# One encoder layer on one core: sums of the down weights formed in the gate/up part and kept in DRAM, operands loaded in pairs, four gate products run ahead, and the norm of the first four token tiles inside the last pass

## Chip, cores and metric

One NeuronCore of a Trainium2 chip runs the whole layer in one launch. The metric is the device time in microseconds; the median of three runs is given beside the lowest and the highest.

## What is computed

The input x is 1024 tokens by 1024 channels in float32. The layer is a half-step SwiGLU, a mixer, another half-step SwiGLU and a last norm:

```
x = x + 0.5 * swiglu(rmsnorm(x, ff1_norm), ff1_w_gate, ff1_w_up, ff1_w_down)
h = rmsnorm(x, mix_norm);  proj = h @ w_in
x = x + merged(gMLP(proj), stick_breaking_attention(proj)) @ w_out
x = x + 0.5 * swiglu(rmsnorm(x, ff2_norm), ff2_w_gate, ff2_w_up, ff2_w_down)
y = rmsnorm(x, final_norm)
swiglu(x, g, u, d) = (silu(x @ g) * (x @ u)) @ d        # d_ff = 2816
```

The change touches the two SwiGLU stages alone, "the first half" (stage f1, whose next consumer is the mixer) and "the second half" (stage f2, whose next consumer is the output).

## The kernel before, in words

Every operand of a matmul is split in two float32r parts, hi (a cast by ACT, L73) and lo (source minus hi by DVE, L74), and each product is three matmuls, hi·hi, hi·lo and lo·hi (`mm3f`, L170 to L172). A pair of such parts of a 128x512 block is a *form* (`form`).

Each SwiGLU stage (`ffn`) multiplies 2x2 blocks by Strassen's scheme in Winograd's form, with seven products instead of eight, and so needs sums and differences of blocks on both sides.

*Prologue* (`right_forms`): eight token tiles of 128 tokens are loaded (xr, two buffers), normed (`normed`, `rstd`), transposed by PE (nt, L203, eight transposes a tile) and written as the right operands B11, B21 (tiles 0 to 3) and T1 to T4, B22 (tiles 4 to 7, differences with tiles 0 to 3, which are kept in `keep`). `rstd` squares on ACT (L105), adds on DVE (L107, L108) and takes the power on POOL (L109). With `offload` one half of the norm is a product on POOL (L116) that ACT scales (L120); the other half is one DVE instruction (L122).

*Gate/up part*: 22 column tiles f of 128 columns. `head(f)` loads 512 KB of gate and of up weights (raw, four buffers) and does the first two products; `tail(f)` does the sums of weights (ws) and the other five, 84 matmuls of 512 columns together. Two heads run ahead. SiLU and the product with up (`gated`) give the activation blocks (act); after every second f, DVE forms the sums S1 to S4 (as, three buffers) and SP writes seven blocks of 256 KB to DRAM.

*Down part*: four passes over 11 pairs j of row blocks. Pass 1 is A11·B11 + A12·B21 in eight PSUM banks (A and B), pass 2 S2·T2 and S1·T1, pass 3 S3·T3 and S4·B22, pass 4 A22·T4 in four banks. Passes 1 to 3 have 24 matmuls per j, pass 4 has 12: 924 in all. The forms live in eight buffers for even j (wf) and eight for odd j (pf). T1 to T4 are formed here, by DVE from rows of the down weights (L367, L368, L381, L400); T2 goes to DRAM after pass 2 and comes back in pass 4. Between passes DVE drains the banks into x (L359, L360, L375, L376, L389 to L391). Then `after(t)` norms the tiles 0 to 3; in the first half it also transposes them for the mixer (L142) and writes x to DRAM. In pass 4 the last five j run token tile by token tile, and each tile is drained (L408) and normed when its bank is done.

```
            def pair(*srcs):
                r = bp.tile([P, D], F32, tag="raw", bufs=4, name="raw")
                for i, src in enumerate(srcs):
                    nc.sync.dma_start(out=r[:, i * HALF:(i + 1) * HALF], in_=src)
                return cut(r)
```

All DMAs stand in one queue, SP's, and each engine takes its instructions in one fixed order. The framework orders them when the program is built, from the order of the code and the buffers that are free; so a line that stands late in the code can stand early in a queue. An instruction that waits holds all behind it on its engine.

Of the kernel before, what the change touches and what calls it, by code (L numbers as in the profile page):

```python
# [32 lines left out]
class Kernel:  # L33
# [78 lines left out]
    def normed(self, x, gain, tiles, offload):  # L112

        nc = self.nc
        if offload:
            nc.gpsimd.tensor_tensor(tiles[1], x[1], gain[1], op=ALU.mult)  # L116
        r = self.rstd(x)
        for i in range(2):
            if offload and i == 1:
# [13 lines left out]
    def norm_t(self, x, t, gain, h, split=True):  # L133
# [4 lines left out]
        self.normed(x[t], gain, xns, split)  # L138
        for i, xn in enumerate(xns):
            ps = self.psum("p2" if split else ("p2", "p1")[i], "nt")  # L140
# [33 lines left out]
    def right_forms(self, xsrc, gain_src, tp):  # L174


        nc, tt = self.nc, self.nc.vector.tensor_tensor
        names = ("B11", "B21", "T2", "T1", "T3", "T4", "B22")
        T = {n: (self.hp if i < 4 else tp).tile([P, 4, 2, HALF], F32R, tag="h", name=n) for i, n in enumerate(names)}
        with self.tc.tile_pool(name="pre", bufs=1, reuse_waits="tile") as pre:  # L180
            tmp = lambda tag, bufs: pre.tile([P, HALF], F32, tag=tag, bufs=bufs, name=tag)
            self.np_ = pre
            xs = []
# [9 lines left out]
            nc.sync.dma_start(out=gain, in_=gain_src.partition_broadcast(P))  # L193
            for t in range(NT):
                x, nxt = nxt, load(t + 1) if t + 1 < NT else None
                xn = [tmp("xn", 3) for _ in range(2)]
                cut = lambda y: [y[:, i * HALF:(i + 1) * HALF] for i in range(2)]
                self.normed(cut(x), cut(gain), xn, t >= 4)
# [7 lines left out]
                r3 = lambda y: y.rearrange("p (k c) -> p k c", k=4)  # L206

                def put(name, src):
                    o = T[name]
                    self.split(o[:, :, 0, c:c + P], o[:, :, 1, c:c + P], r3(src))  # L210

                if t < 4:
                    for i, name in enumerate(("B11", "B21")):
                        put(name, n[i])
                        keep[i, t] = tmp("keep", 8)
                        nc.scalar.copy(keep[i, t], n[i])
                else:
                    t1, t2, t3, t4 = (tmp("t", 3) for _ in range(4))
# [3 lines left out]
                    put("T1", t1)  # L222
                    tt(t2, n[1], t1, op=ALU.subtract)
                    put("T2", t2)
                    tt(t3, n[1], b12, op=ALU.subtract)
                    put("T3", t3)
                    put("B22", n[1])
                    tt(t4, t2, keep[1, t - 4], op=ALU.subtract)
                    put("T4", t4)
        return T  # L230

    def ffn(self, xsrc, gain_src, wg, wu, wd, before, after):

        nc, tc, tt = self.nc, self.tc, self.nc.vector.tensor_tensor
        nff, nj = DFF // P, DFF // P // 2
        aform = {n: self.dram.tile([nj * P, HALF], F32, name=f"{self.stage}_{n}") for n in ("A11", "A12", "A22", "S1", "S2", "S3", "S4")}
        t2dram = self.dram.tile([nj * P, HALF], F32, name=f"{self.stage}_t2")
        with ExitStack() as outer:
            fps = outer.enter_context(tc.tile_pool(name="fps", bufs=8, space=PSUM, reuse_waits="tile"))
            self.psum = lambda tag, name: fps.tile([P, HALF], F32, tag="ps", name=name)  # L240
            bp = outer.enter_context(tc.tile_pool(name="bp", bufs=1, reuse_waits="tile"))


            with tc.tile_pool(name="tp", bufs=3, reuse_waits="tile") as tp:
                T = self.right_forms(xsrc, gain_src, tp)
                with tc.tile_pool(name="pa", bufs=1, reuse_waits="tile") as pa:
                    tile = lambda tag, bufs: pa.tile([P, HALF], F32, tag=tag, bufs=bufs, name=tag)

                    def weights(f):
                        raw = []  # L250
                        for w in (wg, wu):
                            r = bp.tile([P, D], F32, tag="raw", bufs=4, name="raw")
                            nc.sync.dma_start(out=r.rearrange("p (k c) -> p k c", k=NK), in_=w[:, f * P:(f + 1) * P].rearrange("(k p) c -> p k c", p=P))
                            raw += [r[:, :HALF], r[:, HALF:]]
                        return raw
# [7 lines left out]
                    def head(f):  # L263

                        raw = weights(f)
                        b, a = self.psum("ps", "pb"), self.psum("ps", "pa")
                        product(b, raw[0], "B11", True)
                        p1 = tile("pe", 4)
                        nc.scalar.copy(p1, b)
                        product(a, raw[1], "B21", True)  # L270
                        glo = tile("gs", 4)
                        tt(glo, a, p1, op=ALU.add)
                        return raw, b, glo

                    def gated(g, u):

                        s = tile("gs", 4)
# [5 lines left out]
                    def tail(f, raw, b, glo):  # L283
                        a11, a12, a21, a22 = raw
                        s1, s2, s3, s4 = self.sums(lambda: tile("ws", 4), *raw)
                        product(b, s2, "T2", False)
                        w = tile("pe", 4)
# [4 lines left out]
                        v = tile("pe", 4)  # L292
# [8 lines left out]
                        ghi = tile("gs", 4)  # L301
# [3 lines left out]
                    heads = {f: head(f) for f in range(2)}  # L305
                    for f in range(nff):
                        out = tail(f, *heads.pop(f))
                        if f % 2 == 0:
                            even = out
                        else:  # L310
                            j = f // 2
                            blocks = dict(zip(("A11", "A12", "A21", "A22"), (even[0], out[0], even[1], out[1])))
                            blocks |= zip(("S1", "S2", "S3", "S4"), self.sums(lambda: tile("as", 3), *blocks.values()))
                            for n, dst in aform.items():
                                nc.sync.dma_start(out=dst[j * P:(j + 1) * P, :], in_=blocks[n])
                        if f + 2 < nff:
                            heads[f + 2] = head(f + 2)


            with tc.tile_pool(name="pb", bufs=1, reuse_waits="tile") as pb:  # L320
# [3 lines left out]
                cut = lambda y: [y[:, i * HALF:(i + 1) * HALF] for i in range(2)]  # L324
                wdq = lambda j, r, c: wd[(2 * j + r) * P:(2 * j + r + 1) * P, c * HALF:(c + 1) * HALF]
                af = lambda n, j: aform[n][j * P:(j + 1) * P, :]
# [442 lines left out]
```

## Time and profile before

| | us |
|---|---|
| median of 3 runs | 2624.23 |
| lowest, highest | 2623.71, 2625.22 |
| the profiled execution, its own time | 2623.44 |
| its span | 2621.7 |
| PE busy | 2446.7 (93%) |
| DVE busy | 1724.2 (66%) |
| ACT busy | 1054.5 (40%) |
| POOL busy | 306.5 (12%) |

The span is one execution as the profiler saw it, 1.7 us less than the time of the same execution. PE is the busiest engine. Busy time of PE is modelled for pipelined matmuls: a matmul of 512 columns shows some 390 ns, but one issues about every 227 ns. An engine's idle time costs nothing unless the chain of waits runs through it.

### The profile page before, as it was taken

To read this page: it belongs to the slowest core of one execution; us is meant where nothing else is said; L and a number is where in the kernel's file an instruction comes from. 1 tells how busy PE (TensorE), PEld (TensorE's weight loads), DVE (VectorE), ACT (ScalarE), POOL (GpSimd) and SP (SyncE) were. 2 spreads that over 40 slices of the span, in tenths; PEclk is the share of its full clock that TensorE was granted. 3 is DMA by queue.
4 is the path that set the end of the run, shared out by engine and by line. 5 is a ranking of instruction groups with operands and counts; after the bars stand their busy time and mean duration, and the time that the engine had idled before them with its cause. 6 is when DMAs were issued, how large, how long until landed. Compare 5 with 4: busy or idle time off the path is not lost.

```text
span 2621.7 us, 33247 instructions
## 1 busy us (share of the span) xinstructions
PE 2446.7 (93%) x12140; PEld 2073.0 (79%) x12140; DVE 1724.2 (66%) x2641; ACT 1054.5 (40%) x2004; POOL 306.5 (12%) x478
## 2 busy tenths in 40 slices
PE   4999999999689999999999999999959999999987
PEld 3888888787477989888888888888748888887875
DVE  7777676575647888878766555145586766765756
ACT  6333333433335666666522222221063333333334
POOL 1000000000104454544300000000010000000002
PEclk9999999999799999999999999999969999999998
DMA  3332333785422122121121122123232333337754
GB/s 113 97 116 94 99 114 109 269 293 167 138 73 69 43 57 55 43 57 49 33 57 53 47 69 62 56 72 105 98 103 89 121 101 101 101 114 277 264 172 164
DMA packets 258755, 282.67 MB, mean 108 GB/s; under 512 B 16801, under 2 KB 165793, under 8 KB 258593
## 3 DMA queue, kind: packets, MB, share of 16 engines
q1 hardware_dynamic: 258592, 280.56, 33.8%
q8 instruction: 95, 1.56, 0.2%
q14 instruction: 68, 0.55, 0.1%
HBM read 209.20 MB, written 62.91 MB: 104 GB/s over the span
## 4 chain that ended last, share of the span: by engine, by line
PE 75%; DMA 11%; DVE 8%; issue 3%; ACT 2%; SPq 1%; POOL 1%; DVEq 0%; POOLq 0%; ACTq 0%
PE pj L67 7%; PE pj L69 7%; PE pj L68 7%; DMA raw<-in_ff_w_down_dram 6%; PE pb L171 5%; PE pb L170 5%; PE pb L172 5%; PE pd L171 3%; PE pd L170 3%; PE pd L172 3%; PE av L524 3%; PE pv L68 2%; PE pv L69 2%; PE pv L67 2%; PE tr L517 2%
## 5 line engine op out<-in xcount | busy, mean ns | idle before, releaser
L67 PE MATMUL pj<-h,wr 128*128 128x512 f32 x640 | 252.5, 395 | 6.9 <-DVE q L74 6.9
L69 PE MATMUL pj<-h,wr 128*128 128x512 f32 x640 | 250.8, 392 | 0.1
L68 PE MATMUL pj<-h,wr 128*128 128x512 f32 x640 | 250.6, 392 | 0.0
L74 DVE TENSOR_TENSOR wf<-raw,wf 128x512 fp32r<-128x512 f32 x252 | 170.9, 688 | 111.4 <-ACT wf L73 111.0
L73 ACT CAST wf<-raw 128x512 fp32r<-128x512 f32 x252 | 153.0, 621 | 192.8 <-PE pa L172 61.4
L500 DVE TENSOR_TENSOR_SCAN kp<-kp 128x128 f32<-128x128 f32 (+7 forms) x128 | 181.8, 1426 | 44.7 <-POOL kp L498 43.1
L73 ACT CAST wf<-ws 128x512 fp32r<-128x512 f32 x176 | 109.2, 623 | 139.2 <-PE pd L172 128.0
L170 PE MATMUL pd<-wf 128*128 128x512 f32 x336 | 134.8, 401 | 26.1 <-DVE x L375 15.7
L56 DVE TENSOR_TENSOR wr<-raw,wr 128x1024 fp32r<-128x1024 f32 x80 | 97.9, 1223 | 81.8 <-ACT wr L55 81.6
L504 POOL TENSOR_TENSOR bt<-bt,kp 128x512 f32<-128x512 f32 (+4 forms) x128 | 133.8, 1046 | 131.4 <-DVE kp L500 104.8
L67 PE MATMUL pv<-wr,h 128*128 128x256 f32 x512 | 145.9, 287 | 1.9 <-ACT vg L566 1.9
L68 PE MATMUL pv<-wr,h 128*128 128x256 f32 x512 | 145.4, 284 | 0.6 <-DVE wr L56 0.6
L69 PE MATMUL pv<-wr,h 128*128 128x256 f32 x512 | 145.2, 284 | 0.0
L67 PEld LDWEIGHTS pj<-h,wr 128*128 128x128 f32 x640 | 120.6, 189 | 31.0 <-DVE q L74 7.6
L69 PEld LDWEIGHTS pj<-h,wr 128*128 128x128 f32 x640 | 120.5, 188 | 25.2 <-DVE wr L56 0.3
L68 PEld LDWEIGHTS pj<-h,wr 128*128 128x128 f32 x640 | 120.8, 189 | 23.4
L170 PE MATMUL pb<-T,wf 128*128 128x512 f32 x352 | 136.9, 389 | 0.0
L171 PE MATMUL pb<-T,wf 128*128 128x512 f32 x352 | 136.9, 389 | 0.0
L172 PE MATMUL pb<-T,wf 128*128 128x512 f32 x352 | 136.9, 389 | 0.0
L55 ACT CAST wr<-raw 128x1024 fp32r<-128x1024 f32 x80 | 84.2, 1052 | 130.1 <-PE pd L69 53.6
L171 PE MATMUL pd<-wf 128*128 128x512 f32 x336 | 134.0, 399 | 0.3 <-DVE wf L74 0.2
L172 PE MATMUL pd<-wf 128*128 128x512 f32 x336 | 133.2, 398 | 0.0
(210 smaller groups left out, 6488.2 us busy)
## 6 DMA issues: line engine op xcount, KB each, us to landing
raw<-in_ff_w_down_dram SPq DMA_DIRECT2D x132, 256.0 KB, 4.0
raw<-in_w_in_dram SPq DMA_DIRECT2D x56, 512.0 KB, 3.9
raw<-in_ff_w_gate_dram SPq DMA_DIRECT2D x44, 512.0 KB, 5.5
raw<-in_ff_w_up_dram SPq DMA_DIRECT2D x44, 512.0 KB, 4.0
f_S<-as SPq DMA_DIRECT2D x88, 256.0 KB, 2.1
raw<-f_S SPq DMA_DIRECT2D x88, 256.0 KB, 4.2
f_A<-act SPq DMA_DIRECT2D x66, 256.0 KB, 3.3
raw<-f_A SPq DMA_DIRECT2D x66, 256.0 KB, 3.8
```

Source lines behind the costliest of these rows:

```text
L55: nc.scalar.copy(wr[:, 0, :], raw)
L56: (nc.gpsimd if early else nc.vector).tensor_tensor(wr[:, 1, :], raw, wr[:, 0, :].bitcast(F32), op=ALU.subtract)
L67: mm(ps, lhsT=lh, rhs=rh, start=first, stop=False)
L68: mm(ps, lhsT=lh, rhs=rl, start=False, stop=False)
L69: mm(ps, lhsT=ll, rhs=rh, start=False, stop=last)
L73: self.nc.scalar.copy(hi, src)
L74: self.nc.vector.tensor_tensor(lo, src, hi.bitcast(F32), op=ALU.subtract)
L170: mm(ps, lhsT=lh, rhs=rh, start=first, stop=False, skip_group_check=True)
L171: mm(ps, lhsT=lh, rhs=rl, start=False, stop=False, skip_group_check=True)
L172: mm(ps, lhsT=ll, rhs=rh, start=False, stop=last, skip_group_check=True)
L500: nc.vector.tensor_tensor_scan(rev, rev, rev, 1.0, op0=ALU.mult, op1=ALU.bypass)
L504: eng.tensor_tensor(bt[:, :n], bt[:, :n], kp[:, i * HALF + 1:i * HALF + 1 + n], op=ALU.mult)
```

## The change

In the gate/up part, `right_sums(j)` loads two whole down rows after every even f, forms T1 to T4 on DVE and writes them to DRAM; `left_sums(j)` writes S2 with S1 and S3 with S4 as one block of 512 KB each. The DRAM layout puts the two operands that a pass needs together side by side, so that `pair` loads 512 KB at once. Four heads run ahead instead of two; for these the gate weights are loaded a second time, and from f = 4 on a head stands directly ahead of its tail. In the prologue both halves of the norm are DVE's, POOL takes three of five low parts of tiles 4 to 7 and the sum `keep`, which ACT copied before. In the down part the sums are gone, the fourth pass starts ahead of the norm, and the norm of tiles 0 to 3 (both halves offloaded to POOL and ACT) stands inside it.

```diff
@@ normed: offload is now the number of halves that go to POOL and ACT
-        if offload:
-            nc.gpsimd.tensor_tensor(tiles[1], x[1], gain[1], op=ALU.mult)
+        far = [i for i in range(2) if i >= 2 - offload]
+        for i in far:
+            nc.gpsimd.tensor_tensor(tiles[i], x[i], gain[i], op=ALU.mult)
@@ right_forms
-                self.normed(cut(x), cut(gain), xn, t >= 4)
+                self.normed(cut(x), cut(gain), xn, 0)
...
-                        put(name, n[i])
+                        hi, lo = put(name, n[i], tt)
                         keep[i, t] = tmp("keep", 8)
-                        nc.scalar.copy(keep[i, t], n[i])
+                        pt(r3(keep[i, t]), hi, lo, op=ALU.add)
                 else:
...
+                    put("T2", t2, tt)
+                    put("T1", t1, pt)
...
+                    put("T3", t3, pt)
+                    put("B22", n[1], tt)
                     tt(t4, t2, keep[1, t - 4], op=ALU.subtract)
+                    put("T4", t4, pt)
@@ ffn
-        nff, nj = DFF // P, DFF // P // 2
+        nff, nj, nhead = DFF // P, DFF // P // 2, 4
+        scratch = {n: self.dram.tile([nj * P, D], F32, name=f"{self.stage}_{n}") for n in ("a11a12", "s2s1", "s3s4", "a22t4", "t2t1", "t3")}
...
-                    def tail(f, raw, b, glo):
-                        a11, a12, a21, a22 = raw
+                    def tail(f, gate, b, glo):
+                        a11, a12 = weights(wg, f) if f < nhead else gate
+                        a21, a22 = weights(wu, f)
...
+                    def left_sums(j, a11, a12, a21, a22):
+                        s21, s34 = pairs()
+                        self.sums(iter((s21[:, HALF:], s21[:, :HALF], s34[:, :HALF], s34[:, HALF:])).__next__, a11, a12, a21, a22)
+                        for n, i, y in (("a11a12", 0, a11), ("a11a12", 1, a12), ("a22t4", 0, a22), ("s2s1", None, s21), ("s3s4", None, s34)):
+                            nc.sync.dma_start(out=dst(n, j, i), in_=y)
+                    def right_sums(j):
+                        r = [rawt() for _ in range(2)]
+                        for i in range(2):
+                            nc.sync.dma_start(out=r[i], in_=wd[(2 * j + i) * P:(2 * j + i + 1) * P, :])
+                        (b11, b12), (b21, b22) = cut(r[0]), cut(r[1])
+                        t21, t34 = pairs()
+                        (t2, t1), (t3, t4) = cut(t21), cut(t34)
+                        tt(t1, b12, b11, op=ALU.subtract)
+                        tt(t2, b22, t1, op=ALU.subtract)
+                        tt(t3, b22, b12, op=ALU.subtract)
+                        tt(t4, t2, b21, op=ALU.subtract)
+                        for n, i, y in (("t2t1", None, t21), ("t3", 0, t3), ("a22t4", 1, t4)):
+                            nc.sync.dma_start(out=dst(n, j, i), in_=y)
-                    heads = {f: head(f) for f in range(2)}
+                    heads = {f: head(f) for f in range(nhead)}
                     for f in range(nff):
-                        out = tail(f, *heads.pop(f))
+                        out = tail(f, *(heads.pop(f) if f in heads else head(f)))
                         if f % 2 == 0:
                             even = out
+                            right_sums(f // 2)
...
+                def pair(src):
+                    r = rawt() if len(src) == 1 else pb.tile([P, D], F32, tag="rw", bufs=3, name="rw")
+                    for i, y in enumerate(src):
+                        o = r if len(src) == 1 else r[:, i * HALF:(i + 1) * HALF]
+                        nc.sync.dma_start(out=o if len(y.shape) == 2 else o.rearrange("p (r c) -> p r c", r=2), in_=y)
                     return cut(r)
+                two(lambda j: [dst("a11a12", j)], lambda j: [col1(j)], A, B, "AB")
...
+                two(lambda j: [dst("s2s1", j)], lambda j: [dst("t2t1", j)], A, B, "B")
...
+                two(lambda j: [dst("s3s4", j)], lambda j: [dst("t3", j, 0), b22(j)], A, B, "")
...
+                old, A, fs = A, banks(), {}
+                last(range(3), range(4))
                 for t in range(4):
+                    tt(xh(t + 4, 0), old[t], xh(t + 4, 0), op=ALU.add)
+                    tt(xh(t + 4, 1), old[t], xh(t + 4, 1), op=ALU.add)
+                after(0, cut(x[0]), cut(gain), 2)
+                after(1, cut(x[1]), cut(gain), 2)
+                last(range(3, 6), range(4))
+                after(2, cut(x[2]), cut(gain), 2)
+                after(3, cut(x[3]), cut(gain), 2)
+                for t in range(4):
+                    last(range(6, nj), [t], t == 0)
                     tt(xh(t + 4, 0), xh(t + 4, 0), A[t], op=ALU.subtract)
+                    after(t + 4, cut(x[t + 4]), cut(gain), 1)
```

`two` is the loop of passes 1 to 3 with its operands as arguments: `pair` for the left and for the right, four forms, and the 24 matmuls of before. In passes 1 and 2 both loads are whole, in pass 3 the right one is two halves in the pool rw. In the changed kernel the line numbers shift: L388 and L389 drain after pass 2, L395, L407 and L408 after pass 3, L416 after pass 4.

How the queues stand is shown at three places. The first is SP's queue from the start of the first half, ahead of the loads of the gate/up part. Before:

```order
L188 DMA xr<-in_x_dram 128x1024
L193 DMA gain<-in_ff_norm_dram 128x1024
L188 DMA xr<-in_x_dram 128x1024
L253 DMA raw<-in_ff_w_gate_dram 128x8x128
L253 DMA raw<-in_ff_w_up_dram 128x8x128
L253 DMA raw<-in_ff_w_gate_dram 128x8x128
L253 DMA raw<-in_ff_w_up_dram 128x8x128
L676 DMA bgate<-in_b_gate_dram 128x16x1
L188 DMA xr<-in_x_dram 128x1024 x6
```

And of the change:

```order
L188 DMA xr<-in_x_dram 128x1024
L193 DMA gain<-in_ff_norm_dram 128x1024
L188 DMA xr<-in_x_dram 128x1024
L260 DMA raw<-in_ff_w_gate_dram 128x8x128 x4
L684 DMA bgate<-in_b_gate_dram 128x16x1
L188 DMA xr<-in_x_dram 128x1024
L260 DMA raw<-in_ff_w_gate_dram 128x8x128
L260 DMA raw<-in_ff_w_up_dram 128x8x128
L188 DMA xr<-in_x_dram 128x1024
L326 DMA raw<-in_ff_w_down_dram 128x1024 x2
L188 DMA xr<-in_x_dram 128x1024 x4
```

Four more loads of 512 KB stand ahead of token tile 4: the reload of the first gate weights, the first up weights and two down rows. In the second half the reload stands ahead of tile 0, and the up weights and two down rows ahead of tile 2.

The second place is DVE's queue between passes 2 and 3 of the first half; the forms wf and pf with a source raw, wt or rw are those of passes 2 and 3, and L375 and L388 are the drains of bank group A. Before:

```order
L381 TENSOR_TENSOR wt<-raw 128x512
L74 TENSOR_TENSOR pf<-raw,pf 128x512
L74 TENSOR_TENSOR pf<-wt,pf 128x512
L74 TENSOR_TENSOR pf<-raw,pf 128x512 x2
L74 TENSOR_TENSOR wf<-raw,wf 128x512
L74 TENSOR_TENSOR wf<-wt,wf 128x512
L381 TENSOR_TENSOR wt<-raw 128x512
L74 TENSOR_TENSOR wf<-raw,wf 128x512 x2
L74 TENSOR_TENSOR pf<-raw,pf 128x512
L375 TENSOR_TENSOR x<-pd,x 128x512
L376 TENSOR_TENSOR x<-pd,x 128x512
L381 TENSOR_TENSOR wt<-raw 128x512
```

And of the change:

```order
L74 TENSOR_TENSOR pf<-raw,pf 128x512
L74 TENSOR_TENSOR pf<-rw,pf 128x512
L74 TENSOR_TENSOR wf<-raw,wf 128x512
L74 TENSOR_TENSOR wf<-rw,wf 128x512
L74 TENSOR_TENSOR wf<-raw,wf 128x512
L74 TENSOR_TENSOR wf<-rw,wf 128x512
L74 TENSOR_TENSOR pf<-raw,pf 128x512
L74 TENSOR_TENSOR pf<-rw,pf 128x512
L388 TENSOR_TENSOR x<-pd,x 128x512
L74 TENSOR_TENSOR pf<-raw,pf 128x512
L389 TENSOR_TENSOR x<-pd,x 128x512
L74 TENSOR_TENSOR pf<-rw,pf 128x512
```

The subtractions L381 are gone from the queue ahead of the drains and between them, and the forms of two j of pass 3 stand ahead of the first drain.

The third place is PE's queue in the first half around the first transposes of the norm (nt). Before, they stand between pass 3 and pass 4:

```order
L170 MATMUL pd<-wf 128x512
L171 MATMUL pd<-wf 128x512
L172 MATMUL pd<-wf 128x512
L142 MATMUL nt<-ident,xn 128x128 x32
L170 MATMUL pd<-wf 128x512
L171 MATMUL pd<-wf 128x512
```

And of the change:

```order
L173 MATMUL pd<-pf 128x512
L171 MATMUL pd<-pf 128x512
L143 MATMUL nt<-ident,xn 128x128 x8
L172 MATMUL pd<-pf 128x512
L173 MATMUL pd<-pf 128x512
L171 MATMUL pd<-wf 128x512
```

The eight transposes of tile 0 now stand behind 67 matmuls of pass 4; those of tiles 1 to 3 follow within the next 49, and those of tiles 4 to 7 stand behind its last matmul.

## Rows read from the trace of the kernel before

**Rows 1.** Windows: us, busy of PE, PEld, DVE, ACT, POOL, PEclk, DMA share, GB/s.
```profile
0.00:52.00 52.00, 15.46 (x64) 12.43 (x65) 36.35 (x66) 34.96 (x75) 10.94 (x18) 1.00 0.45 132
52.00:475.50 423.50, 423.50 (x1865) 350.61 (x1864) 296.24 (x470) 157.08 (x274) 0.00 (x0) 1.00 0.33 104
475.50:749.00 273.50, 226.70 (x978) 185.99 (x977) 170.93 (x272) 110.20 (x207) 15.63 (x16) 0.90 0.63 212
1895.00:1948.60 53.60, 15.46 (x64) 12.45 (x65) 37.19 (x67) 33.91 (x74) 10.21 (x12) 0.53 0.43 138
1948.60:2372.00 423.40, 423.40 (x1862) 350.56 (x1861) 296.18 (x470) 155.77 (x273) 0.00 (x0) 1.00 0.32 103
2372.00:2621.70 249.70, 216.34 (x913) 175.63 (x912) 159.92 (x254) 99.18 (x188) 15.75 (x16) 0.93 0.65 223
```

**Rows 2.** Timeline of PE: start, length, instruction, idle before and its ender.
```profile
483.84 0.79 PE L171 MATMUL pd<-pf 128*128 128x512 f32 x1 [3.52 <-DVE pf L74]
607.04 0.76 PE L170 MATMUL pd<-wf 128*128 128x512 f32 x1 [6.28 <-DVE x L375]
689.92 1.97 PE L142 MATMUL nt<-ident,xn 128*128 128x128 f32 x8 [20.95 <-DVE xn L122]
2578.33 0.76 PE L170 MATMUL pd<-wf 128*128 128x512 f32 x1 [8.81 <-DVE x L389]
```

**Rows 3.** Waits of PE: waited for, us in total, times, longest.
```profile
PE pd L170 <- DVE x L375: 15.7, 2, 9.5
```

**Rows 4.** Chain of waits, pass 4, first half: start, us, what.
```profile
702.88 0.43 PE pd L170
706.89 0.23 PE pd L171
```

**Rows 5.** Timeline of DVE at the starts of pass 1 and pass 3.
```profile
481.89 0.69 DVE L165 TENSOR_TENSOR as<-act,as 128x512 f32<-128x512 f32 x1 [1.42 <-DMA f_S<-as]
600.94 0.69 DVE L381 TENSOR_TENSOR wt<-raw 128x512 f32<-128x512 f32 x1 [3.25 <-DMA raw<-in_ff_w_down_dram]
606.21 0.69 DVE L375 TENSOR_TENSOR x<-pd,x 128x512 f32<-128x512 f32 x1
606.81 0.68 DVE L376 TENSOR_TENSOR x<-pd,x 128x512 f32<-128x512 f32 x1
```

**Rows 6.** Timeline of PE in the prologues: one token tile's transposes.
```profile
36.93 1.94 PE L203 MATMUL nt<-ident,xn 128*128 128x128 f32 x8 [3.81 <-DVE xn L122]
44.19 1.94 PE L203 MATMUL nt<-ident,xn 128*128 128x128 f32 x8 [5.32 <-DVE xn L122]
50.43 1.94 PE L203 MATMUL nt<-ident,xn 128*128 128x128 f32 x8 [4.31 <-DVE xn L122]
1947.01 1.94 PE L203 MATMUL nt<-ident,xn 128*128 128x128 f32 x8 [4.30 <-DVE xn L122]
```

**Rows 7.** Timeline of DVE and of POOL, late token tiles of the first prologue.
```profile
30.29 0.74 DVE L122 SCALAR_TENSOR_TENSOR xn<-xr,rs,gain 128x512 f32<-128x512 f32 x1
35.02 1.76 DVE L122 SCALAR_TENSOR_TENSOR xn<-xr,rs,gain 128x512 f32<-128x512 f32 x1
34.62 1.61 POOL L116 TENSOR_TENSOR xn<-xr,gain 128x512 f32<-128x512 f32 x1
```

**Rows 8.** Timeline of PE at the end of the two halves.
```profile
735.33 1.03 PE L142 MATMUL nt<-ident,xn 128*128 128x128 f32 x8
746.64 1.97 PE L142 MATMUL nt<-ident,xn 128*128 128x128 f32 x8 [4.42 <-DVE xn L122]
2612.04 0.39 PE L172 MATMUL pd<-wf 128*128 128x512 f32 x1
```

**Rows 9.** DMA issues: queue, count, KB each, median us from issue to landing.
```profile
raw<-in_w_in_dram SPq DMA_DIRECT2D x56, 512.0 KB, 3.9
raw<-f_S SPq DMA_DIRECT2D x88, 256.0 KB, 4.2
```

**Rows 10.** View by windows, pass 1 while x is loaded.
```profile
490.00:540.00 50.00, 49.56 (x219) 40.73 (x217) 27.61 (x44) 21.46 (x38) 0.00 (x0) 1.00 0.95 325
```

More of the change, by code (lines that the diff above doesn't have):

```diff
@@ L241, in ffn @@
             bp = outer.enter_context(tc.tile_pool(name="bp", bufs=1, reuse_waits="tile"))
+            rawt = lambda: bp.tile([P, D], F32, tag="raw", bufs=4, name="raw")
             with tc.tile_pool(name="tp", bufs=3, reuse_waits="tile") as tp:
@@ L247, in ffn, with weights @@
                     tile = lambda tag, bufs: pa.tile([P, HALF], F32, tag=tag, bufs=bufs, name=tag)
[L249 to L255, printed above, removed]
+                    def weights(w, f):
+                        r = rawt()
+                        nc.sync.dma_start(out=r.rearrange("p (k c) -> p k c", k=NK), in_=w[:, f * P:(f + 1) * P].rearrange("(k p) c -> p k c", p=P))
+                        return cut(r)
                     def product(ps, src, right, first, last=True):
@@ L263, in head @@
                     def head(f):
-                        raw = weights(f)
+                        gate = weights(wg, f)
                         b, a = self.psum("ps", "pb"), self.psum("ps", "pa")
-                        product(b, raw[0], "B11", True)
-                        p1 = tile("pe", 4)
+                        product(b, gate[0], "B11", True)
+                        p1 = tile("pe", 3)
                         nc.scalar.copy(p1, b)
-                        product(a, raw[1], "B21", True)
-                        glo = tile("gs", 4)
+                        product(a, gate[1], "B21", True)
+                        glo = tile("gs", 6)
                         tt(glo, a, p1, op=ALU.add)
-                        return raw, b, glo
+                        return gate, b, glo
                     def gated(g, u):
-                        s = tile("gs", 4)
+                        s = tile("gs", 6)
                         nc.scalar.activation(s, g, AF.Sigmoid)
@@ L300, in tail, with pairs @@
                         lo = gated(glo, ulo)
-                        ghi = tile("gs", 4)
+                        ghi = tile("gs", 6)
                         tt(ghi, d, w, op=ALU.add)
                         return lo, gated(ghi, uhi)
-                    heads = {f: head(f) for f in range(2)}
+                    def pairs():
+                        return [pa.tile([P, D], F32, tag="as", bufs=3, name="as") for _ in range(2)]
+                    def left_sums(j, a11, a12, a21, a22):
[3 more added lines that the diff above has]
+                            nc.sync.dma_start(out=dst(n, j, i), in_=y)
```

133 lines of the change are left out of this document (41 added, 92 removed).

## Prediction, made before the changed kernel ran

> **What bounds the kernel now.** I read the stages first. In both gate/up parts PE is busy all of the time, 423.5 us of 423.5 for 1865 recorded matmuls, so a matmul of 512 columns issues every 0.227 us [rows 1]. These parts can't get shorter while their matmuls stay. PE's losses lie elsewhere: two prologues of some 52 us, in which PE does 15.5 us of transposes, and two down parts of 273.5 and 249.7 us [rows 1] that hold 924 matmuls each, 924 x 0.227 = 209.7 us.
>
> PE's timeline names the holes of the down parts [rows 2]. At the start of pass 1 it idles 3.5 us for the low part of a form. At the start of pass 3 it idles 6.3 us for a bank that DVE has not drained (L375), and 9.5 us in the second half, since the two waits sum to 15.7 [rows 3]. Ahead of pass 4 it idles 21.0 us in the first half, for the norm of token tile 0, whose transposes stand ahead of pass 4 in PE's queue, and 8.8 us in the second, where nothing is transposed [rows 2]. After a hole the matmuls issue every 0.43 us for some ten of them before they return to 0.23 [rows 4]: some 10 x 0.20 = 2 us more each time. That is the lower level of the granted clock, 1.2 GHz for 2.4.
>
> Why DVE is late shows in its own timeline [rows 5]. The drain L375 at 606.21 stands behind L381, a subtraction that waited 3.25 us for a row of down weights. The sum L165 waited 1.42 us for the write of an earlier sum out of the same three buffers. So transfers bound these starts, through DVE's queue. A 512 KB load lands in 3.9 us, a 256 KB one in 4.2 [rows 9]: two halves cost more than one whole.
>
> **Removed: the sums in passes 2 to 4.** L381 and its like leave DVE's queue; pass 3's operands are one whole load and two halves prefetched in a pool of three. The DVE order shows two tiles' forms ahead of the drains now, 48 matmuls or 10.9 us of cover, and nothing there waits for raw down weights to be subtracted. Both holes go: 6.3 + 9.5, and 2 of slow matmuls each, **-19.8 us**. Bounds: 0 if the paired loads come as late, 19.8 if they don't.
>
> **Moved: the norm of the first four tiles.** In the first half pass 3 ends at 689.92 - 20.95 = 668.97, and the last transposes end at 746.64 + 1.97 = 748.6 [rows 2, 8], 79.6 us later. In the new order pass 4 needs only the drains of B, which begin before pass 3 ends; I allow 1.5 us. Its 132 matmuls take 30.0 us, four tiles' transposes at 1.03 each 4.1 [rows 8], and the tail from 735.33 on stays, 13.3 [rows 8]: 48.9, a gain of 30.7. In the second half the old stretch runs from 2578.33 - 8.81 = 2569.5 to 2621.7, 52.2 us [rows 2]. The new one is 1.5 + 30.0 and the tail after the last matmul, 2621.7 - 2612.4 = 9.3 [rows 8]: 40.8, a gain of 11.4. The norm's price is that it now runs beside the forms. It brings twelve POOL products into the pass. One such product, 1.61 us at 34.62, goes with a DVE instruction of 1.76 us at 35.02 that takes 0.74 alone [rows 7], so each may cost DVE 1.0 us: 0 to 12 us per half. I take 3, since tile 0's transposes stand behind 67 matmuls (15 us of cover): **-27.7 and -8.4 us**.
>
> **Start of pass 1.** The 1.42 us wait for the sum's buffer goes, but only 6 matmuls stand between the last gate/up product and the first form of the next tile. The sigmoid, two products and four sums still come first on DVE. I take **-2 us** for both halves (bounds 0 and 11: 3.5 of idle time and 2 of slow matmuls each).
>
> **Added: sums of down weights in the gate/up part.** Forty-four subtractions per half, 44 x 0.60 = 26 us of DVE at the interval between 606.21 and 606.81 [rows 5], where DVE is busy 296 of 423.5 us [rows 1]. In the steady stretch it is 70% and becomes 76%, hidden. But after four early pairs of products come four tails of 60 matmuls, 13.6 us each, and such a tail costs DVE 16 instructions plus 4 sums, 20 x 0.60 = 12.0 us: 88%, where a late transfer has little slack. I take **+2 us** per half (bounds 0 and 6). The traffic grows by 2 MB per pair of columns in 38 us, far under the 325 GB/s that pass 1 sustains [rows 10].
>
> **Prologues.** Running four pairs ahead gains nothing by itself: in both orders all 64 transposes stand ahead of the first product, and PE does not idle after it [rows 1]. What counts is when the last transposes run, 50.43 and 1947.01 [rows 6]. A late tile takes 7.26 us now (36.93 to 44.19), on DVE. It then has eight DVE instructions of 0.60 and two short ones for the statistics, some 5.1 us, and POOL three subtractions at up to 1.61 us [rows 7] and the power. If POOL never holds DVE the three periods save 3 x 2 = 6 us; if each of its three does for 1.0, a period is 8.2 and they lose 3. I take 7.0. Against it, SP's order puts a reload, the up weights and two down rows, 2 MB or 6.5 us at 325 GB/s [rows 10], ahead of the x tile 4 that starts this stretch; in the second half three of the four. I take **+3 and +1 us** (bounds -6 and +9 each).
>
> The Trainium skill (SBUF — State Buffer, Who interferes with whom) states that a DVE instruction with two SBUF inputs and a GpSimd instruction that reads SBUF shut each other out for the whole instruction. The 1.76 against 0.74 [rows 7] agrees, and the rule speaks against moving subtractions to POOL: four of DVE's eight still have two SBUF inputs. By it these four and the three of POOL run one after the other, 4 x 0.60 + 3 x 1.61 = 7.2 us a tile, so the sum would be 3 x 0.2 = 0.6 us longer per prologue than by my 7.0.
>
> **The sum.** -19.8 - 27.7 - 8.4 - 2 + 4 + 4 = -49.9. The profiled execution took 2623.4 us (span 2621.7), 0.8 under the median of the three runs. I predict **2573.5 us**.
>
> **Rivals.** *One: the prologue becomes POOL's and SP's.* If every POOL subtraction shuts out DVE, a period is 8.2 or more and the x tiles come 6.5 us later, so each prologue ends 9 us late: 2573.5 + 14 = 2587.5. For it: rows 7, and the order of SP. Against it: most POOL subtractions can run beside drains from PSUM. Chance 0.18. *Two: the norm within pass 4 makes PE wait.* If its twelve POOL products cost DVE 12 us per half, and PE stops at the transposes, 18 us of the 36 are lost: 2591.5. Against it: the cover of 15 us. Chance 0.13. *Three, slower: the sums wait in the gate/up part.* Each of the 22 groups of subtractions needs two down rows that SP issues behind writes which wait for DVE; all forms stand behind the subtractions. If each group stops PE, it costs about a landing of 4.2 us [rows 9], 22 x 4.2 = 92: 2666. It turns the sign from 50 / 22 = 2.3 us of stall per group on. Against it: four load buffers and 24% of DVE free. Chance 0.06. *Four: the change doesn't do what it says,* because paired loads come as late as halves did and the drains stand behind them; then the 19.8 stays, and with a half of the pass-4 gain gone too the time is 2611. Chance 0.06. My forecast has 0.57.
>
> **How the numbers follow.** Forecast, rivals one, two and four are faster: 0.94, less 0.03 for the parts of one, two and four in which further losses stack, of which 0.02 is no change and 0.01 slower. A measurement of this kernel tells 0.2% from no change, 5 us. So faster 0.91, same 0.02, slower 0.07. The range starts where all bounds of the down parts go well and the prologues save 3 each: 2573.5 - 6 (norm) - 4 (pass 1) - 10 (prologues as above, -3 for +3 and +1) = 2553. It ends above rivals one and two, at 2604, with part of rival four outside.
>
> **What would show it.** PE's wait for L375's successor L388 near zero; the idle time before pass 4 under 2 us in both halves; PE 100% busy in the gate/up parts; the prologues' last transposes at about 53 and 50 us after their start. The prediction is wrong if PE waits for DVE in the gate/up parts, if the transposes inside pass 4 are preceded by idle time, or if the prologues end later than 60 us.

## The result and the profile after

The changed kernel takes 2588.89 us (median of 4 runs, 2588.20 to 2589.35), the kernel before in the same comparison 2624.72 (2623.71 to 2626.21). The ratio is 0.9863, with a 95% interval of 0.9846 to 0.988: 1.4% faster, 36 us where 50 were forecast. The profiled execution has a span of 2587.6 us (2621.7 before).

Busy time by stage of the kernel after, each stage from one mark to the next (columns as in [rows 1]). The marks are the first product of the gate/up part, the matmul that ends the wait for the first low part in pass 1, the first matmul of the mixer and its last:

```profile
core 0: us, PE busy (x) PEld busy (x) DVE busy (x) ACT busy (x) POOL busy (x), PEclk, DMA share, GB/s
0.00:63.26 63.26, 15.95 (x64) 12.17 (x65) 45.79 (x68) 30.74 (x68) 29.44 (x31) 1.00 0.47 141
63.26:495.83 432.57, 428.44 (x1879) 353.18 (x1877) 322.23 (x514) 162.46 (x279) 4.58 (x3) 1.00 0.48 158
495.83:719.93 224.10, 215.31 (x960) 177.88 (x961) 130.83 (x214) 105.54 (x200) 20.34 (x20) 0.96 0.62 214
719.93:1872.04 1152.11, 1132.45 (x6406) 991.55 (x6404) 728.02 (x1046) 463.62 (x916) 259.93 (x416) 0.99 0.20 58
1872.04:1941.07 69.03, 16.30 (x66) 12.16 (x65) 48.01 (x68) 29.88 (x67) 27.87 (x25) 0.53 0.44 137
1941.07:2373.43 432.36, 428.24 (x1878) 353.13 (x1876) 321.85 (x514) 160.91 (x278) 4.59 (x3) 0.99 0.48 158
2373.43:2587.60 214.17, 205.71 (x896) 169.76 (x896) 118.48 (x196) 95.39 (x183) 20.32 (x20) 0.98 0.61 214
```

The same marks in the kernel before give the table that the rest of this text uses; each column is one profiled execution. The forecast column sorts the prediction's terms into these stages (1 us of the -2 for pass 1 goes to each gate/up part; +3 and +1 to the prologues; -8.3 and -11.5 of the -19.8 to the two down parts).

| stage | before | after | difference | forecast |
|---|---|---|---|---|
| prologue 1 | 52.0 | 63.3 | +11.2 | +3 |
| gate/up 1 and start of pass 1 | 431.8 | 432.6 | +0.8 | +1 |
| rest of down part 1 | 264.4 | 224.1 | -40.3 | -36.0 |
| mixer | 1146.2 | 1152.1 | +5.9 | 0 |
| prologue 2 | 54.1 | 69.0 | +14.9 | +1 |
| gate/up 2 and start of pass 1 | 432.4 | 432.4 | 0.0 | +1 |
| rest of down part 2 | 240.7 | 214.2 | -26.5 | -19.9 |
| sum | | | -34.1 | -49.9 |

The down parts gave more than forecast. The loss lies in the prologues, and in a stage that the change doesn't touch. PE's longest waits after (engine, line, releaser: total, times, longest) answer to [rows 3] and [rows 2]:

```profile
PE nt L204 <- DVE xn L123: 100.0, 22, 17.0
PE nt L143 <- DVE xn L123: 7.8, 3, 4.0
PE pd L172 <- DVE pf L74: 5.5, 2, 2.7
PE pd L171 <- ACT pf L73: 2.1, 2, 1.1
```

No drain stands in the list any more: the holes of 6.3 and 9.5 us at the start of pass 3 and of 8.8 us ahead of pass 4 are gone. The prologue's wait for the norm (L204) grew instead, from 74.8 to 100.0 us. PE's timeline of the changed kernel holds these idle times in the first down part, and no other but one of 0.95 us ahead of the last transposes:

```profile
491.89 1.20 PE L171 MATMUL pd<-pf 128*128 128x512 f32 x4 [1.06 <-ACT pf L73]
495.83 0.80 PE L172 MATMUL pd<-pf 128*128 128x512 f32 x1 [2.74 <-DVE pf L74]
...
707.29 1.07 PE L143 MATMUL nt<-ident,xn 128*128 128x128 f32 x8 [1.03 <-DVE xn L123]
712.37 1.97 PE L143 MATMUL nt<-ident,xn 128*128 128x128 f32 x8 [4.02 <-DVE xn L123]
717.13 1.09 PE L143 MATMUL nt<-ident,xn 128*128 128x128 f32 x4 [2.79 <-DVE xn L123]
```

From 496 to 705 us PE never stops, so the transposes inside pass 4 wait for nothing; those from 707 us on stand behind its last product. In the second half PE has no idle time from 2373.4 us to its last product. The 21 us ahead of pass 4 [rows 2] are gone too.

### The profile page after: what moved, and what is told of

Read it like the earlier page. It is cut to its first block, busy times and chain, and to the rows that moved or that the text cites. A ratio compares the mean times of both kernels' runs of the same rounds, so it can differ in the third digit from the quotient of the medians.

```text
span 2587.6 us, 33119 instructions
## 1 busy us (share of the span) xinstructions
PE 2442.4 (94%) x12140; PEld 2069.8 (80%) x12140; DVE 1715.2 (66%) x2617; ACT 1048.5 (41%) x1988; POOL 367.1 (14%) x518
## 4 chain that ended last, share of the span: by engine, by line
PE 58%; DVE 2%; ACT 1%; issue 1%; POOL 1%; DMA 1%; SPq 0%; POOLq 0%; DVEq 0%; ACTq 0%
PE pj L67 6%; PE pj L69 6%; PE pj L68 6%; PE pd L172 4%; PE pd L173 4%; PE pd L171 4%; PE pb L171 2%; PE pb L172 2%; PE pb L173 2%; PE av L532 2%; PE pv L68 2%; PE pv L69 2%; PE pv L67 2%; PE tr L525 2%; PE pa L68 1%; PE pa L67 1%
## 5 line engine op out<-in xcount | busy, mean ns | idle before, releaser
L73 ACT CAST wf<-raw 128x512 fp32r<-128x512 f32 x276 | 164.7, 621 | 301.0 <-PE pd L173 105.0
L74 DVE TENSOR_TENSOR wf<-raw,wf 128x512 fp32r<-128x512 f32 x276 | 183.9, 688 | 142.8 <-ACT wf L73 142.7
L508 DVE TENSOR_TENSOR_SCAN kp<-kp 128x128 f32<-128x128 f32 (+7 forms) x128 | 181.5, 1423 | 46.5 <-POOL kp L506 45.1
L74 DVE TENSOR_TENSOR wf<-ws,wf 128x512 fp32r<-128x512 f32 x176 | 120.0, 687 | 24.7 <-ACT wf L73 24.4
L172 PE MATMUL pd<-wf 128*128 128x512 f32 x336 | 131.4, 391 | 0.0
L173 PE MATMUL pd<-wf 128*128 128x512 f32 x336 | 131.0, 391 | 0.0
```

What stands on the lines that cost most here:

```text
L73: self.nc.scalar.copy(hi, src)
L74: self.nc.vector.tensor_tensor(lo, src, hi.bitcast(F32), op=ALU.subtract)
L172: mm(ps, lhsT=lh, rhs=rl, start=False, stop=False, skip_group_check=True)
L173: mm(ps, lhsT=ll, rhs=rh, start=False, stop=last, skip_group_check=True)
L508: nc.vector.tensor_tensor_scan(rev, rev, rev, 1.0, op0=ALU.mult, op1=ALU.bypass)
```

## Experiments

Three things were open: what lengthened the prologues, why the mixer takes 5.9 us more, and which part of the change made the gain in the down parts. All experiments are read by the stages of the table. The comparisons ran on several chips and single times differ between them (the kernel before took 2617.2 in its one run beside e5 to e8, and 2623.4 beside e1 to e4), so for e2 to e8, which have one time each, the stages carry the argument. The stages of the kernel before are those of one execution of 2623.4 us, and its runs spread from 2617.2 to 2627.6: a sum of differences against them can be off by some 6 us.

### The prologue

**e1**, the old prologue in the changed kernel: `right_forms` as before, the rest as changed. Besides the three edits shown, the order of the splits of T1 and T2 and the number of buffers (xn and t, three for four) are the old ones again.

```
-                        pt(r3(keep[i, t]), hi, lo, op=ALU.add)
+                        nc.scalar.copy(keep[i, t], n[i])
...
-                    put("T1", t1, pt)
+                    put("T1", t1)
...
-                self.normed(cut(x), cut(gain), xn, 0)
+                self.normed(cut(x), cut(gain), xn, int(t >= 4))
```

> The changed kernel with the prologue's arithmetic as it was before (copies for keep on ACT, all low parts on DVE, half a norm on POOL from tile 4 on); loads and heads stay as changed. Now the first prologue takes 63.3 us from the span's start to the first product and the second 69.0 us from the mixer's last matmul (52.0 and 54.1 before). Theory A (the work moved to POOL lengthened them): 53 and 55, time 2588.9 - 24 = 2565. Theory B (SP's weight loads ahead of the x tiles lengthened them): 61 to 63 and 66 to 69, time 2583 to 2589.

Measured: **2557.97 us** (2557.15 to 2558.93), 0.9753 of the kernel before (0.9736 to 0.9769). Prologues of 51.95 and 56.1 us (stages from mark to mark, columns as above):

```profile
0.00:51.95 51.95, 15.26 (x65) 12.60 (x65) 37.64 (x71) 37.06 (x79) 11.08 (x18) 1.00 0.58 172
1855.53:1911.65 56.12, 15.84 (x66) 12.44 (x65) 39.84 (x71) 36.39 (x78) 10.25 (x12) 0.52 0.54 169
```

Theory A holds. Of the 30.4 us between the profiled executions 24.2 lie in the prologues and 5.1 in the mixer, of which no theory spoke (below). The loads that SP issues ahead of the x tiles are still there and cost the first prologue nothing. The second stays 2.0 us over the kernel before, all of it ahead of its first transposes (PE waits 16.9 us for them, 14.9 before).

**e2**, only `keep` back on ACT (the first of the three edits).

> The changed kernel with only the eight keep tiles copied by ACT again; the three low parts of the late tiles stay on POOL. Theory A: in the first four tiles POOL's power no longer stands behind a keep (1.0 us) and DVE's pair of norm instructions takes 1.4 instead of 2.4 us, so tiles 1 to 4 come each some 2 us sooner: prologues 56 and 62, time 2588.9 - 14 = 2575. Theory B: loads set the pace of the first tiles, no change over 1 us.

Measured: 2576.1 us, prologues 58.3 and 61.7, 5.0 and 7.3 less. The changed kernel's DVE and POOL, and then those of e2, show why (start, duration, engine, line; idle time before in brackets):

```profile
32.82 0.15 DVE L108 TENSOR_SCALAR rs<-rs 128x1 f32<-128x1 f32 x1
...
34.52 2.40 DVE L123 SCALAR_TENSOR_TENSOR xn<-xr,rs,gain 128x512 f32<-128x512 f32 x2 [0.79 <-POOL rs L109]
...
32.72 1.26 POOL L218 TENSOR_TENSOR keep<-B 128x512 f32<-128x512 f32 x1 [3.20 <-DVE B L211]
33.94 0.55 POOL L109 TENSOR_TENSOR rs<-rs,neghalf 128x1 f32<-128x1 f32 x1
34.46 1.26 POOL L218 TENSOR_TENSOR keep<-B 128x512 f32<-128x512 f32 x1
```

```profile
29.60 0.15 DVE L108 TENSOR_SCALAR rs<-rs 128x1 f32<-128x1 f32 x1
...
30.48 1.41 DVE L123 SCALAR_TENSOR_TENSOR xn<-xr,rs,gain 128x512 f32<-128x512 f32 x2
...
29.89 0.55 POOL L109 TENSOR_TENSOR rs<-rs,neghalf 128x1 f32<-128x1 f32 x1 [3.84 <-DVE rs L108]
```

In the changed kernel the power for tile 4 (33.94) stands behind a keep that began at 32.72, though its input was there at 33.0: 1 us. Then the second keep runs beside the two norm instructions, which take 2.40 us together and 1.41 in e2: another 1 us. An early tile takes 6.2 us with the keeps on POOL and 4.4 without, by PE's transposes of two tiles in a row, first here, then in e2:

```profile
30.21 1.94 PE L204 MATMUL nt<-ident,xn 128*128 128x128 f32 x8 [4.26 <-DVE xn L123]
36.41 1.94 PE L204 MATMUL nt<-ident,xn 128*128 128x128 f32 x8 [4.27 <-DVE xn L123]
```

```profile
26.98 1.94 PE L204 MATMUL nt<-ident,xn 128*128 128x128 f32 x8 [2.45 <-DVE xn L123]
31.38 1.94 PE L204 MATMUL nt<-ident,xn 128*128 128x128 f32 x8 [2.45 <-DVE xn L123]
```

**e3**, only the late tiles back (the other two edits).

> The changed kernel with only the late tiles put back (three low parts on DVE, half a norm on POOL); the keep sums stay on POOL. Theory A: the late period goes from 8.2 back to 7.3 us, four tiles, so 3 to 4 us less in each prologue: 59.5 and 65.5, time 2582. Theory B: nothing over 1 us.

Measured: 2572.4 us, prologues 58.7 and 65.5: 4.6 and 3.6 less. 5.6 us of the time is the mixer (below). e2 and e3 together give 9.5 and 10.9 of the 11.3 and 12.9 us that e1 gives. The late tiles of the changed kernel, PE's transposes, then DVE, then POOL:

```profile
44.48 1.09 PE L204 MATMUL nt<-ident,xn 128*128 128x128 f32 x4 [6.13 <-DVE xn L123]
...
52.66 1.09 PE L204 MATMUL nt<-ident,xn 128*128 128x128 f32 x4 [5.40 <-DVE xn L123]
...
60.84 1.08 PE L204 MATMUL nt<-ident,xn 128*128 128x128 f32 x4 [5.41 <-DVE xn L123]
```

```profile
42.67 3.36 DVE L123 SCALAR_TENSOR_TENSOR xn<-xr,rs,gain 128x512 f32<-128x512 f32 x2
...
48.02 0.68 DVE L227 TENSOR_TENSOR t<-nt,b 128x512 f32<-128x512 f32 x1
48.62 1.03 DVE L230 TENSOR_TENSOR t<-t,keep 128x512 f32<-128x512 f32 x1
...
42.53 2.95 POOL L211 TENSOR_TENSOR T<-t,T 128x512 fp32r<-128x512 f32 x2
47.84 1.27 POOL L211 TENSOR_TENSOR T<-t,T 128x512 fp32r<-128x512 f32 x1 [2.36 <-ACT T L210]
```

The three late periods, from the transposes at 36.41 on, are 8.07, 8.18 and 8.18 us, 24.4 together. In the kernel before they are 5.75, 7.26 and 6.24, 19.3 together ([rows 6], and the start of the first here):

```profile
31.18 1.94 PE L203 MATMUL nt<-ident,xn 128*128 128x128 f32 x8 [2.15 <-DVE xn L122]
```

So 5.2 of the first prologue's 11.2 us lie here; the 7.3 of the expectation is the longest of the three, not what a late tile takes. In e3 the periods are 5.75, 8.97 and 5.72.

The norm's pair takes 3.36 us beside two POOL subtractions. The lines at 48.02 and 48.62 are the finest reading: while one POOL subtraction runs from 47.84 to 49.11, the DVE instruction with one operand in PSUM (nt) takes its usual 0.68. The one with both in SBUF takes 1.03 and ends at 49.65, 0.54 us after POOL does; the same line takes 0.68 one tile before (at 39.72), with POOL idle.

The Trainium skill (SBUF — State Buffer, Who interferes with whom) states just this difference: two SBUF inputs on DVE contend with a GpSimd instruction that reads SBUF, one does not. The rows agree.

**e4**, two heads ahead instead of four (`nhead = 2`).

> The changed kernel with two heads ahead instead of four: the gate rows of four columns and their reloads no longer stand between the x tiles in SP's queue. Theory A: prologues within 1 us of 63.3 and 69.0, time 2588 to 2590. Theory B: up to 6.5 us less in the first and 5 in the second: 57 and 64, time 2577. Any stall of PE in the gate/up parts (none now) would show what four heads are good for.

Measured: 2581.3 us, but prologues of 63.3 and 68.9, as theory A had it. Both gate/up parts take 431.5 us, some 1 us less, but so they do with four heads in e3 and e5 (431.4 to 431.6), so this is not the heads' doing. The four heads buy nothing. The rest of the difference is the mixer again, 1146.3 us.

### The mixer

The framework orders each engine's instructions when the program is built, and a change in one place shifts its choices in others. DVE and PE in the changed kernel, some 197 us into the mixer, and then DVE in e1 (L508 and L507 are the same line of code):

```profile
916.77 2.29 DVE L508 TENSOR_TENSOR_SCAN kp<-kp 128x1024 f32<-128x1024 f32 x1 [0.18 <-POOL kp L506]
919.09 1.30 DVE L74 TENSOR_TENSOR q<-pj,q 64x512 fp32r<-64x512 f32 x2
...
919.84 0.50 PE L67 MATMUL pj<-h,wr 128*128 128x512 f32 x1 [1.92 <-DVE q L74]
...
921.27 0.63 PE L69 MATMUL pj<-h,wr 128*128 128x512 f32 x1
```

```profile
905.14 1.30 DVE L74 TENSOR_TENSOR q<-pj,q 64x512 fp32r<-64x512 f32 x2
906.47 2.29 DVE L507 TENSOR_TENSOR_SCAN kp<-kp 128x1024 f32<-128x1024 f32 x1
```

The long scan stands ahead of the two low parts of q here, behind them in e1. PE waits 1.92 us for the first of them, and from 920.9 on its matmuls take 0.63 instead of 0.39 us. The stretch just behind, in the columns of [rows 1], shows the granted clock at its lower level, 1.2 GHz:

```profile
921.93:922.93 1.00, 1.00 (x3) 0.76 (x3) 1.00 (x3) 0.00 (x0) 0.00 (x0) 0.50 0.00 0
```

It stays there for some 3 us. The wait and the slow matmuls come to about 1.9 + 1.5 = 3.4 us. Lined up by every 24th of PE's transposes (tr), the changed kernel and e1 are within 0.3 us of each other for the first 186 us of the mixer. At 232 us the changed kernel is 4.9 us behind; then the lag goes down and up again, is 4.7 us at 550, and 5.1 at the end. So nearly all of the difference opens in the 46 us around this place; what makes up the part beyond the 3.4 was not followed further.

**e9** tested this, the prologue of e1 with two heads:

> The old prologue of the first experiment, and two heads ahead instead of four. Two heads cost nothing before, so prologues 52 and 54 to 56, gate/up parts 431.5 each. Theory on the mixer: its time follows the framework's order of DVE alone. In this kernel one 1024-wide scan of the mixer stands ahead of the two low parts of q that PE waits for, as in the changed kernel, so the mixer takes 1152 us, not 1146 to 1147: time 2558 - 1 + 5 = 2560 to 2563, no gain. Rival (the mixer's 6 us depend on the POOL work of the changed prologue): 1146.5, time 2554 to 2557.

Measured: 2564.84 us (2561.76 to 2565.33), mixer 1151.5. The rival falls. The time is 2 us over the range, with gate/up parts of 432.3 and 432.1, not 431.5. Over all runs the scan stands ahead in the changed kernel, e2 and e9 (1152.1, 1152.5, 1151.5 us), and behind in the kernel before, e1 and e3 to e8 (1145.8 to 1147.3). e10 lies between (1148.6, scan behind), but lined up in the same way it is 1.5 us behind e1 after 104 us already, and 1.8 at 229, so its extra does not come from this place. No run changes this order and nothing else: that it is the cause rests on the place where the time is lost and on three kernels against nine.

**e10**, three buffers for the x tiles, the low parts of q ahead:

> The old prologue, two heads, and three buffers for the x tiles of the prologue instead of two. Here the two low parts of q stand ahead of the scan, so the mixer takes 1146 to 1147. The third tile no longer waits behind the gate weights and the second drain of a buffer: if loads hold the first tiles back, they come up to 4 us sooner in each half, prologues 48 and 51, time 2546 to 2550; if the chain of ACT, DVE and POOL sets their pace, 51 to 52 and 54 to 55, time 2553 to 2556.

Measured: 2562.0 us (2560.4 to 2565.9), prologues 50.4 and 57.1. A miss: against e9 one prologue gained 1.6 us and the other lost 1.4, so the loads hold the tiles back by little. The mixer missed its range too, and the first down part took 227.8 us, 3.1 more than in e9, with 3.6 us of waits of PE for the drain at L382. e1 has the lowest time, but against the kernel before e9 and e10 (0.9773 and 0.9769) do not differ from it (0.9753) beyond the intervals.

### The down parts

**e5**, the norm and all drains ahead of pass 4 again:

```
+                    tt(xh(t + 4, 0), A[t], xh(t + 4, 0), op=ALU.add)
+                    tt(xh(t + 4, 1), A[t], xh(t + 4, 1), op=ALU.add)
+                    after(t, cut(x[t]), cut(gain), 1)
...
-                last(range(3), range(4))
...
+                last(range(6), range(4))
```

> The changed kernel with the old start of pass 4: all drains and the norm of token tiles 0 to 3 ahead of its first product, one half of each norm on POOL. The two down parts, from the first product after the wait for the low part to the next stage, take 224.1 and 214.2 us now (264.4 and 240.7 before). Theory: the move of the norm is worth all of that difference but the holes at the start of pass 3 and their slow matmuls (8.3 and 11.5), so they become 256 and 229. The framework's order puts the two low parts of q ahead of the long scan in the mixer, as it was before, so the mixer takes 1146 us again (1152 in the changed kernel). Time 2588.9 - 6 + 32 + 15 = 2630. Rival (the hole ahead of pass 4 went because the loads come sooner): down parts 224 and 214, time 2583.

Measured: 2606.6 us, down parts 243.5 and 218.7, so the move is worth 19.4 and 4.5, not 32 and 15. Neither theory fits. Most of the hole ahead of pass 4 stays away without the move. DVE in the kernel before, at the end of pass 3, then in e5 its first and last drain of B, and PE's hole in e5:

```profile
673.00 0.69 DVE L400 TENSOR_TENSOR wt<-raw,rw 128x512 f32<-128x512 f32 x1 [1.88 <-DMA raw<-f_t]
...
674.81 0.69 DVE L390 TENSOR_TENSOR x<-pd,x 128x512 f32<-128x512 f32 x1
...
683.32 0.69 DVE L389 TENSOR_TENSOR x<-pd,x 128x512 f32<-128x512 f32 x1
```

```profile
668.36 0.68 DVE L395 TENSOR_TENSOR x<-pd,x 128x512 f32<-128x512 f32 x1
...
674.47 0.68 DVE L395 TENSOR_TENSOR x<-pd,x 128x512 f32<-128x512 f32 x1
...
680.13 1.97 PE L143 MATMUL nt<-ident,xn 128*128 128x128 f32 x8 [9.36 <-DVE xn L123]
```

Before, L400, the T4 subtraction of pass 4, had been put ahead of the drains, and waited for t2 to come back from DRAM. Pass 3 ended at about 669 us [rows 2] and the drains ran from 674.8 to 684.0. In e5 pass 3 ends at about 671, and the drains of B begin before that and end at 675. The hole is 9.4 us instead of 21.0; in the second half, where no transposes stand there, it is 0.8 instead of 8.8. So more than half of it came from what e5 keeps of the change, sums and pairs, and only the rest from the norm.

**e6**, the other way round: the kernel before with the move alone (half of each norm stays DVE's here, which the change gives to POOL and ACT too).

> The kernel before with one part of the change alone: the drains of A and the norm of token tiles 0 to 3 stand behind the first three and first six pairs of pass 4. Theory: the move alone gives 32 us in the first half and 15 in the second, down parts of 232 and 226, the holes at the start of pass 3 stay at 6.3 and 9.5 us; time 2624 - 47 = 2577. Rival: DVE, which still subtracts T4 there, feeds pass 4 late, and PE waits for half of it: 2600.

Measured: 2600.0 us, down parts 249.5 and 231.7: 14.9 and 9.0 less, 23.9 in all. The rival's time is met, although the kernel before beside it took 2617.2 us, from which the gain is 17. PE's waits in e6:

```profile
PE pd L170 <- DVE x L375: 14.3, 2, 8.4
PE pd L170 <- DVE x L405: 12.3, 2, 8.2
PE nt L142 <- DVE xn L122: 10.7, 4, 5.7
```

L405 is a drain of A. In the code it stands behind the first three pairs of pass 4, but the first product of pass 4 waits for it, 8.2 us in the first half and 4.1 in the second: ahead of it on DVE stands a T4 subtraction (L397), which in the first half waited 3.02 us for t2.

**e7**, the sums back in the down part, left operands still paired, the norm still inside pass 4 (`right_sums` is left out, and passes 2 to 4 load rows of the down weights and subtract, as before).

> The changed kernel with the sums of down weights formed in the down part again, from rows loaded there; the left operands still come in pairs and the norm stays inside pass 4. Theory A (the sums in DVE's queue made the holes at the start of pass 3): the holes of 6.3 and 9.5 us return with 2 us of slow matmuls each, down parts of 232 and 226; the gate/up parts are at most 1 us shorter; the mixer takes 1146 us; time 2588.9 - 6 + 20 - 1 = 2602. Rival (the pairing removed them): 224 and 214, time 2583.

Measured: 2625.6 us, down parts 247.6 and 233.5: 23.5 and 19.4 more, twice what theory A gave. The gate/up parts are 0.8 and 1.2 us shorter, but e5, with the sums in them, has them 1.0 and 0.8 shorter too. Its waits:

```profile
PE pd L171 <- DVE x L419: 12.0, 2, 6.6
...
PE pd L171 <- DVE x L390: 8.7, 2, 6.0
```

L390 drains A after pass 2, L419 drains it after pass 3. The sums make both late, not only the first.

**e8**, all transfers unpaired, sums in the gate/up part.

```
+                    if len(src) == 1:
+                        y = src[0]
+                        src = [y[:, i * HALF:(i + 1) * HALF] for i in range(2)] ...
```

> The changed kernel with every paired transfer of the down part, and the paired writes of sums, split again in two of 256 KB; the sums stay in the gate/up part. Theory A: no hole returns, down parts within 2 us of 224 and 214, the mixer at 1146, time 2583 to 2586. Rival (pairing is needed, a half lands in 4.2 us where a whole takes 3.9): the holes of 6.3 and 9.5 us return, time 2602.

Measured: 2592.4 us, down parts 230.7 and 219.3, 6.6 and 5.1 more. Between the two. The holes of pass 3 do not return, but a smaller one opens between passes 1 and 2, where L385 drains A:

```profile
PE pd L171 <- DVE x L385: 8.5, 2, 4.3
```

From the kernel before to e5, sums and pairing are worth 20.9 + 22.0 = 42.9 us, and from e5 to the changed kernel the move 19.4 + 4.5 = 23.9. That these two make the 66.8 us of the down parts is so by construction, as e5 lies between the two kernels. The test is in the other runs: without the sums moved (e6) the move is worth 23.9 as well, and with the norm moved the sums are worth 42.8 (e7), so in the total the two hardly depend on each other. By halves they do (14.9 and 9.0 in e6), so the exact agreement is partly chance. Pairing is worth 11.7 with the sums moved. Without that it is worth nothing: e7 and e6 both have the move and form the sums in the down part, e7 with paired left operands and e6 without, and their down parts take 481.1 and 481.2 us together.

## Why the prediction was right or wrong

The time lies in the range, and the sign is right. 2573.5 was 15.4 us too low. Rival one gave 2587.5 and had a chance of 0.18; half of its mechanism is what happened: POOL's subtractions hold DVE, and a late period is 8.2. Its other half, x tiles 6.5 us late, is not, and the `keep` tiles are missing in it. That it agrees within 2 us is luck: the prologues lost 26.1 us where it said 18, the mixer took 5.9 more, and the down parts gave 10.9 more.

*Prologues, +3 and +1: wrong, measured +11.2 and +14.9.* Three steps failed. The first is the list of what moved: the eight `keep` tiles that went from ACT to POOL have no term at all, neither for the power behind them nor for the norm beside them, and e2 prices them at 5.0 and 7.3 us. The second is "A late tile takes 7.26 us now": that is the longest of three periods, which take 19.3 us together. From there, three of 8.2 lose 5.3 us, not 3, and three of 7.0 lose 1.7, where against 7.26 they would gain 0.8. The third is "I take 7.0" for the new period. The bound of 8.2, which the text itself had worked out for the case that each POOL subtraction holds DVE, is what was measured, and the sign of error that the text named, a prologue of over 60 us, is in the first row of the stages. (The 50 us named for the last transposes of the second prologue fit no row: they stood 52.5 us after the mixer's last matmul, and +1 gives 53.5. The last tile's transposes began 60.8 and 66.6 us after the start of their prologues.) The choice between the bounds went against the row that was nearest, 1.76 us for 0.74 [rows 7]. The sentence with the rule's own sum, 7.2 us, was low too: it leaves out what else stands in a tile's chain, PE's transposes, the statistics and POOL's power. The price for SP's queue was wrong the other way: e1 and e4 show nothing of it in the first prologue, and at most 2 us in the second.

*Removed sums, -19.8, and moved norm, -27.7 and -8.4: the sum of 55.9 was low, 66.8, and divided wrongly.* The runs give 42.9 for sums and pairs and 23.9 for the move. The step that failed is "Moved": it took the whole stretch from 668.97 to the last transposes as the norm's doing. The release by DVE xn in [rows 2] names the last link only; ahead of it on DVE stood the T4 subtraction that waited for DRAM, and the drains behind it. The same mistake in the second half gave 8.4 for a move that is worth 4.5 in the finished kernel. The new stretches themselves were sized well: with the end of pass 3 placed as in e5, 175.8 us behind the mark (an estimate), they take 48.7 and 38.4 us, for 48.9 and 40.8 in the text. That pass 4 needs only the drains of B does not hold in general: in e6 and e7 its first product waits for a drain of A (L405, L419). The 3 us for POOL's products within pass 4 and the 1.5 for the drains were not needed: PE has no idle time there, so rival two is false. The 2 us of slow matmuls after each hole were right in kind, and the hole ahead of pass 4 in the second half had them too, which I did not count.

*Start of pass 1, -2: right.* The idle times fell from 1.34 and 3.52 to 1.06 and 2.74, 1.06 us per half. *Gate/up, +2 per half: near in size, not by its cause.* From the first product to the first idle time of pass 1, PE takes 427.6 and 427.4 us, 425.8 and 426.3 before: 1.8 and 1.0 more. The sums are not shown to be the reason: the stage takes 431.6 in both halves of e5, with them, and 431.8 and 431.1 in e7, without. PE shows no wait for the new subtractions, and DVE is busy for 322 of 432.6 us, 74% (76% forecast). Rival three is false. Rival four is false as well: the paired loads do come in time, and e8 shows that halves would not quite.

*Not in the prediction: +5.9 in the mixer.* The prediction compared the orders only where the change is.

## What to carry to other kernels

A wait's releaser is the last link: before a hole is put down to the step that ended it, look at what stood ahead of that step on its engine and what that waited for; that decides which of two edits gets the gain. Work moved to POOL beside DVE instructions with two SBUF inputs is not removed from DVE's path, and what POOL must do next (here a power of one element per partition) waits as well. And when a framework orders the instructions, compare the order of the stages that the change does not touch, too: here one pair of instructions behind a scan goes with 5 to 6 us, a sixth of what the change gained. A price per tile is read over all tiles of its kind: the 7.26 us taken here were the longest of 5.75, 7.26 and 6.24.

## What the runs showed of the hardware

The contention of DVE and POOL was expected as a possibility; its form was not. Two norm instructions took 1.41, 2.40 and 3.36 us beside none, one and two POOL instructions of 128x512, about 1 us for each. In the same stretch a DVE instruction with an operand in PSUM took 0.68 us beside POOL, unchanged. What share the POOL subtractions and the norm that came back to DVE each have in e3's 4.6 and 3.6 us was not tried apart.
